# Which engine waits for the last stores: five semaphore waits moved from SP to TensorE at the end of an RMSNorm kernel

## Chip, cores and metric

One core of one Trainium2 chip. The metric is the device time of one execution in microseconds (us); lower is better. The groups of experiments ran on different chips, each together with the kernel before, so times are compared within a group; the short intervals that are read from traces are compared across groups as well.

Terms: the span is the time from the first to the last instruction of the program. A store has landed when the last of the 16 increments of its semaphore has come. In the lines of the profile, SPq, ACTq, DVEq and PEldq are the instruction queues of SP, ScalarE, VectorE and TensorE, and POOL is GpSimd.

## The reference

```python
def reference(x, gamma, eps):          # x: (16, 1024, 512) float32, gamma: ones(512), eps 1e-5
    rms = np.sqrt(np.mean(x ** 2, axis=-1, keepdims=True) + eps)
    x_norm = x / rms * gamma
    return np.maximum(x_norm, 0).astype(np.float32)
```

33.55 MB are read and 33.55 MB written, with little arithmetic on each element.

## The kernel before

Each of 128 partitions has 128 rows of 512 numbers. SP issues all 9 loads of x and all 7 stores, each with a semaphore of its own (`sems[m]`). GpSimd waits for the loads and passes the word on to ScalarE, which sums squares and takes the root; VectorE divides, scales and clips. TensorE computes nothing. Behind all work the semaphores that the program used are waited for and brought back to zero (a cut of the kernel; the comments are added here):

```python
    L, S = 0, 1
    room = nslots * K                                   # 6 * 16 = 96 rows of buffer
    order = [(L, 0, G), (L, G, G)] + [(L, i * K, K) for i in range(1, nslots)] + [
        (S, 0, K), (S, K, K), (L, room, K), (L, room + K, K),
        (S, 2 * K, 2 * K), (S, 4 * K, 2 * K), (S, room, K),
        (S, room + K, G), (S, room + K + G, G)]         # (kind, first row, rows); K = 16, G = 8
    # ... cut
    def take(engine, sem, n):
        engine.wait_ge(sem, n)
        engine.sem_inc(sem, -n)                         # built as one instruction: wait and subtract
    # ... cut: loads, stores, arithmetic
    take(nc.sync, done, ngroups)
    take(nc.sync, tick, ndyn)
    take(nc.sync, sq, ngroups - ndyn)
    take(nc.sync, sv, steps)
    take(nc.sync, sem_g, 16)
    for m, (kind, a, r) in enumerate(order):
        if kind == S and a + room >= rows:              # rows = 128: stores from row 32 on
            take(nc.sync, sems[m], 16)
```

The condition holds for five of the seven stores. The two earlier ones are waited for by SP before it reuses their buffers.

## Time and profile before

| kernel before | |
|---|---|
| time, median of 3 | 159.94 us (159.9 to 160.0) |
| span, first to last instruction | 158.6 us |
| time less span, profiled run | 1.32 us |
| DMA queue of SP | 98.6% of 16 engines' span, 67.11 MB |
| VectorE / ScalarE busy | 85% / 54% |
| last store: landing, SP's wait starts, ends | 158.563, 158.579, 158.596 us |

Transfers fill the span, so the span is set by them. The 1.32 us behind the span is the other part of the time, and the part that this change is about. The page doesn't show it, as no instruction of the program runs there. The trace's semaphore updates do. In what follows, "the walk" is a chain of nine steps of one semaphore that the trace lists (in the kernel before from 2.595 to 158.897 us): five up, read as the engines' reports, one after another, that they are through, and four back, read as the engines being let go in the reverse order. The trace doesn't name the engine of a step; what the reading rests on stands behind the prediction. There are two walks behind the kernel (the second from 159.682 to 160.039). "Resets" is the name for what lies between them: one more update each of over 200 semaphores, from 158.854 to 159.458 us; what these updates write is not recorded.

### The profile page before, as it was taken

What the parts mean: (1) busy time and instruction counts of PE and PEld (TensorE: products, weight loads), DVE (VectorE), ACT (ScalarE), POOL (GpSimd) and SP (SyncE); (2) the same over time, 40 slices, a digit from 0 to 9 for tenths busy, and PEclk for the clock granted to TensorE, in tenths of its full rate; (3) what the DMA queues carried; (4) which work ended last, traced back from release to release, by engine and by line L of the source; (5) the groups of instructions that cost most, each with busy time, mean ns of one, the idle gap of its engine ahead of it and who ended that gap; (6) DMA issues with size and microseconds to landing.
All of it is one profiled execution on the core that took longest, in us unless ns stands there. A gap on an engine that the chain in (4) does not pass through costs nothing.

```text
span 158.6 us, 770 instructions
## 1 busy us (share of the span) xinstructions
DVE 135.2 (85%) x76; ACT 86.3 (54%) x273; POOL 0.8 (0%) x6
## 2 busy tenths in 40 slices
DVE  0014999999999999999979999999999999999910
ACT  0388929889889989988920098898600000000000
POOL 1000000000000000000000000000000000000000
DMA  6999999999999999999999999997969969999997
GB/s 190 411 450 422 512 397 397 463 463 397 405 504 413 397 413 504 405 397 463 463 397 397 446 479 397 529 463 331 529 298 496 529 264 529 397 397 397 455 405 331
DMA packets 2312, 67.12 MB, mean 423 GB/s; under 512 B 260, under 2 KB 260, under 8 KB 264
## 3 DMA queue, kind: packets, MB, share of 16 engines
q1 hardware_dynamic: 2304, 67.11, 98.6%
q10 hardware_dynamic: 8, 0.01, 0.0%
HBM read 33.56 MB, written 33.55 MB: 423 GB/s over the span
## 4 chain that ended last, share of the span: by engine, by line
DVE 44%; ACT 27%; issue 6%; ACTq 4%; DVEq 0%; POOLq 0%
ACT junk L131 26%; DVE slots L185 22%; DVE slots L168 22%; ACTq L131 3%; ACTq L126 1%; DVE rstd L168 0%; ACT rms L136 0%; ACTq L136 0%; ACTq L139 0%; DVEq L181 0%; POOLq L118 0%
## 5 line engine op out<-in xcount | busy, mean ns | idle before, releaser
L131 ACT ACTIVATE junk<-slots 128x512 f32 x128 | 74.4, 581 | 21.7 <-POOLq L118 17.2
L185 DVE CUSTOM_DVE_ANT_1 slots<-slots,gamma_sb 128x8192 f32<-128x8192 f32 (+1 forms) x6 | 43.5, 7269 | 0.6
L168 DVE TENSOR_TENSOR slots<-slots,rstd 128x8192 f32<-128x8192 f32 x5 | 43.4, 8689 | 0.1
L154 DVE SCALAR_TENSOR_TENSOR slots<-slots,rstd,gamma_sb 128x512 f32 x48 | 32.3, 747 | 0.9 <-DVE rstd L149 0.9
L131 ACT ACTIVATION_READ_ACCUMULATOR junk<-slots x128 | 23.9, 187 | 0.0
L161 DVE TENSOR_SCALAR slots<-slots x6 | 13.8, 2294 | 0.2
L142 DVE LOAD_MASK_SELECT gamma_sb<-gseed x1 | 0.0, 14 | 8.2 <-DMA gseed<-in_gamma_dram 8.2
L136 ACT ACTIVATE rms<-ss,eps_sb x16 | 4.8, 301 | 1.8
L149 DVE RECIPROCAL rstd<-rms x6 | 1.2, 196 | 5.1 <-ACT rms L136 5.1
L124 ACT ACT_TABLE_LOAD x1 | 1.3, 1283 | 4.0 <-issue 4.0
L168 DVE RECIPROCAL rstd<-rms 128x32 f32<-128x32 f32 (+1 forms) x3 | 0.9, 315 | 0.9 <-ACT rms L136 0.9
L142 DVE STREAM_SHUFFLE gamma_sb<-gseed 128x512 f32<-128x512 f32 x1 | 0.7, 721 | 0.0
L113 POOL MEMSET gseed<- 128x512 f32 x1 | 0.5, 524 | 1.9 <-POOLq L98 1.9
L214 POOL MEMSET const-uint8-127<- 128x1 uint8 x1 | 0.1, 102 | 0.0
L214 POOL MEMSET const-bfloat16-1.0<- 128x1 bf16 x1 | 0.1, 101 | 0.0
L214 POOL MEMSET const-float32-0.0<- 128x1 f32 x1 | 0.1, 98 | 0.2 <-issue 0.2
L114 POOL MEMSET eps_sb<- 128x1 f32 x1 | 0.1, 99 | 0.0
L214 POOL MEMSET const-float32-1.0<- 128x1 f32 x1 | 0.1, 98 | 0.0
## 6 DMA issues: line engine op xcount, KB each, us to landing
slots<-in_x_dram SPq DMA_DIRECT2D x7, 4096.0 KB, 29.6
out_dram<-slots SPq DMA_DIRECT2D x3, 4096.0 KB, 15.0
slots<-in_x_dram SPq DMA_DIRECT2D x2, 2048.0 KB, 9.5
out_dram<-slots SPq DMA_DIRECT2D x2, 2048.0 KB, 7.1
out_dram<-slots SPq DMA_DIRECT2D x2, 22.2
gseed<-in_gamma_dram ACTq DMA_DIRECT2D x1, 8.0 KB
```

The costliest lines, as they stand in the source:

```text
L113: nc.gpsimd.memset(gseed, 0.0).then_inc(sem_z, 1)
L124: nc.scalar.preload_act_table(ACTF.Sqrt)
L126: with nc.scalar.Fori(0, ngroups) as gi:
L131: a = nc.scalar.activation(out=junk[:, j, :], in_=slots[:, bass.ds(base + j * d, d)], func=ACTF.Square, accum_out=ss[:, bass.ds(col + j, 1)])
L136: nc.scalar.activation(out=rms[:, bass.ds(col, G)], in_=ss[:, bass.ds(col, G)], func=ACTF.Sqrt, bias=eps_sb, scale=inv_d).then_inc(sq, 1)
L142: nc.vector.stream_shuffle(gamma_sb, gseed, [0] * 32)
L149: nc.vector.reciprocal(out=rstd[:, bass.ds(col, G)], in_=rms[:, bass.ds(col, G)]).then_inc(sv, 1)
L154: r = nc.vector.scalar_tensor_tensor(out=row, in0=row, scalar=rstd[:, bass.ds(col + j, 1)], in1=gamma_sb, op0=ALU.mult, op1=ALU.mult)
L161: nc.vector.tensor_scalar_max(out=blk, in0=blk, scalar1=0.0).then_inc(done, 1)
L168: emit(**kw).then_inc(sv, 1)
L185: nc.vector._custom_dve(dve_ops.TENSOR_MUL_SAT, out=blk, in0=blk, in1=gamma_sb[:, None, :].to_broadcast([P, r, d]), s0=float("inf"), s1=0. ...
L214: nc = _bacc.Bacc("TRN2", target_bir_lowering=False, num_devices=1)
```

## The change

Its intent: SP, which issues the transfers, is rid of the last waits, and TensorE, which has nothing to do, takes them. (The words that came with it speak of two stores; five waits move.)

```diff
     take(nc.sync, sem_g, 16)
     for m, (kind, a, r) in enumerate(order):
         if kind == S and a + room >= rows:
-            take(nc.sync, sems[m], 16)
+            take(nc.tensor, sems[m], 16)
```

## The prediction

> **What bounds the kernel now.** I read three things in order: the page, to see which engine or queue is full; the groups of instructions by line, to see what the moved waits are and how long each takes; and the trace's list of semaphore updates, to see what still runs after the last instruction of the program. The time before is 159.94 us (median of 3, 159.9 to 160.0), the profiled run took 159.92 us, and its span from first to last instruction is 158.6 us.
>
> The page, first the slices and the queues, then the issues:
>
> ```profile
> span 158.6 us, 770 instructions
> DVE 135.2 (85%) x76; ACT 86.3 (54%) x273; POOL 0.8 (0%) x6
> ...
> DVE  0014999999999999999979999999999999999910
> ...
> DMA  6999999999999999999999999997969969999997
> ...
> q1 hardware_dynamic: 2304, 67.11, 98.6%
> ...
> out_dram<-slots SPq DMA_DIRECT2D x2, 2048.0 KB, 7.1
> ```
>
> The DMA row is full nearly from end to end, and the queue that SP issues on is busy for 98.6% of the span over 16 engines: 67.11 MB at 423 GB/s is 158.6 us. VectorE, the next busiest, has 85% and does nothing in the last slice. TensorE has no row at all: it does no work. So the transfers set the time, and at the very end it is one transfer, the last 2 MB store. The stretches of the end show it:
>
> ```profile
> core 0: us, DVE busy (x) ACT busy (x) POOL busy (x), PEclk, DMA share, GB/s
> ...
> 142.50:151.20 8.70, 8.65 (x2) 0.00 (x0) 0.00 (x0) 1.00 0.96 414
> 151.20:158.60 7.40, 0.00 (x0) 0.00 (x0) 0.00 (x0) 1.00 0.85 363
> ```
>
> From 151.2 us on nothing computes; only bytes move, for 7.4 us. What waits for them is SP, in the line that the helper for "wait and subtract" has. The waits of SP's queue in the last 9 us, then the durations of that line, and of the barrier line at the start, the only place where TensorE runs an instruction of the same kind:
>
> ```profile
> SPq L87 <- SPq L87: 6.5, 2, 4.9
> ...
> L87 SPq EVENT_SEMAPHORE  x12: 17/17/17, 71.2 to 158.6; - x12
> ...
> L98 SPq EVENT_SEMAPHORE  x2: 17/17/17, 2.0 to 2.3; - x2
> ...
> L98 PEldq EVENT_SEMAPHORE  x2: 51/51/51, 2.0 to 2.3; - x2
> ```
>
> In the first line SP waits for 6.5 us in two pieces, the longest 4.9 us: these are the two last stores. (The view names SP's own line as the releaser since SP issued those stores.) The other lines give the price of one wait-and-subtract: 17 ns on SP, 51 ns on TensorE.
>
> **After the last instruction.** The time is 1.32 us longer than the span (159.92 less 158.6). The trace's semaphore updates go on there, and I read them one by one. The last increments of the last store's semaphore come at 158.563; SP's wait starts at 158.579 and ends at 158.596. Then a semaphore that the program does not use is stepped: at 2.595, 113.911, 113.949, 151.299, 158.733, and at once back at 158.776, 158.814, 158.849, 158.897. Nine steps are five engines going up and four coming back. The first five match the times at which the engines run out of instructions: TensorE ends at 2.360, ScalarE at 113.763, GpSimd long before ScalarE, VectorE at 151.148, SP at 158.596. So the order is TensorE, ScalarE, GpSimd, VectorE, SP, and back; each must wait for the one ahead of it, and TensorE is let go last. After it come the resets of about 50 semaphores an engine (158.854 to 159.458; the last block, starting at 159.11, is the slow one, TensorE's), and a second walk of nine steps, from 159.682 to 160.039.
>
> [...]
>
> **The change part by part.** The words speak of two stores, but the condition (a + 96 at least 128) holds for five: the stores from rows 32, 64, 96, 112 and 120. So five waits leave SP and five appear on TensorE. No engine's transfers, arithmetic, or order of issue change, and no byte moves earlier or later.
>
> 1. Removed on SP: five instructions of 17 ns, about 67 ns apart. Four of them were past by 153.745, waiting for data, and only the last lies on the end: 16 ns from landing to start, and 17 ns of execution.
> 2. Added on TensorE: it is through with the opening barrier at 2.36 us and then parks on the first of the five semaphores. Those fill at about 119.8, 139.1, 148.8, 153.7 and 158.56 us, so again only the last is on the end. It starts at about 158.59: in the opening barrier TensorE woke 11 ns later than SP (0.661 against 0.650), so I add 11 to SP's 158.579. It ends 51 ns later, 158.64. The span should thus read 158.64, 0.045 more.
> 3. From the last instruction to the engine's step in the walk: SP needed 0.137 (158.596 to 158.733), TensorE 0.235 (2.360 to 2.595). TensorE steps at about 158.876.
> 4. The walk. Before, the late engine was the last of the chain: the way up was done and only the way back was left, 0.164 us (158.733 to 158.897). Now the late engine is the first: all of the way up is still to do, then the way back. The whole walk is seen twice in this trace with nobody late: the second one behind the kernel, 159.682 to 160.039, is 0.357 us, and the last one before it, from -0.371 to 0, is 0.371. I take 0.364. The walk ends at 159.240 in place of 158.897.
> 5. What follows (resets, second walk) is the same and starts 0.343 later.
>
> Sum: (0.011 + 0.034) for the instruction, (0.235 - 0.137) = 0.098 for the way to the step, and (0.364 - 0.164) = 0.200 for the walk; together 0.343 us. 159.94 + 0.34 = 160.28 us, 0.2% slower.
>
> **Rivals.** (a) The walk is not in what is timed, or is not ordered as I read it: then only the slower instruction remains, +0.05 us, 159.99. For it: the page shows nothing of the walk. Against it: the time exceeds the span by 1.32 us, about what the walks and resets take. (b) SP, freed of its waits, is done at 151.9 and something starts earlier: a gain. Against it: SP has no store left to issue after 151.5, and the transfers end when the bytes have moved, so 159.94 or less by nothing. [...] (c) TensorE wakes slowly out of a wait of over 100 us, or the five waits delay each other. For it: it is the slowest sequencer here, 51 ns against 17. Against it: the last two stores land 4.8 us apart and the five cost well under 1 us if all were taken in a row; a slow wake of 0.5 us would make 160.8. (d) A last wait of another engine takes over. None can: the other engines end by 151.9.
>
> **Range and chances.** My point is 160.28. The low end, 160.0, takes in rival (a) with the scatter of 0.1 that the three runs show; the high end, 160.5, takes in 0.2 for a slower way from TensorE's last wait to the barrier[...]. Two per cent is 3.2 us, ten times the sum, and no part of the change reaches the transfers, so within 2% has 0.985, slower 0.01, faster 0.005.
>
> **What would show it.** Right: TensorE's sequencer has five more entries on the helper's line, 51 ns each, the last at about 158.59; SP's last entry is near 151.86; the span is 0.03 to 0.1 longer while the time grows by about 0.34, so that time less span goes from 1.3 to about 1.6; the step semaphore has its nine steps close together within 0.4 us after 158.8, rather than strung out from 2.6; the DMA rows and the busy times of VectorE and ScalarE stay within 0.3 us. Wrong: the first step still comes early (then TensorE is not the first of the walk), the time grows by no more than the span does (rival a), or TensorE's last wait starts over 0.1 us after the landing (rival c). If the stores themselves landed at another time, the change would act through the transfers, which nothing here foresees.

A paragraph and two single passages with statements that no trace of this case shows are cut out of the prediction. No term of its sum goes with them: 0.045 for the instruction, 0.098 for the way to the step and 0.200 for the walk are 0.343 us, and 159.94 + 0.34 is 160.28.

What its reading of the walk and the resets rests on, from the traces of before and of the changed kernel:

- The five steps up are put to the engines by the ends of their instructions, as the prediction says. That each waits for the one ahead shows in GpSimd, whose last instruction ends at 100.443 and whose step comes at 113.949, 0.038 us behind ScalarE's.
- The four steps back are put to VectorE, GpSimd, ScalarE and TensorE by the time from the step ahead: 0.043, 0.038 and 0.035 us for the first three, as those engines have on the way up in the second walk (0.044, 0.038 and 0.034).
- In the kernel before, the steps of the two walks that follow on at once are 23 to 48 ns apart, but for the turn behind SP's step in the second walk, 99 ns. In the changed kernel's first walk, where VectorE had made its own step only 24 ns ahead of SP's, the turn takes 97 ns; in the first walk of before, where VectorE's step was at 151.299, 43 ns.
- The resets come in five runs of consecutive semaphores, 42 to 49 of each recorded in the kernel before and 47 to 51 in the changed one. They begin 0.121, 0.151, 0.140, 0.116 and 0.213 us behind the fifth to ninth step of the first walk; in the changed kernel, where these steps lie otherwise, 0.117, 0.149, 0.141, 0.115 and 0.215. So each run of resets is put to the engine of its step. TensorE's takes 0.348 us, SP's 0.087.
- SP's last wait lasted 4.9 us and is recorded with 17 ns.
- From the last landing (158.563) to the time of the profiled run (159.92) are 1.36 us: 0.33 to the end of the first walk, 0.56 to the end of the resets, the rest most of the second walk.

## The result

| | before | changed |
|---|---|---|
| median, us | 159.97 (159.9 to 160.29, 6 runs) | 160.38 (160.26 to 160.62, 6 runs) |
| ratio | | 1.0025 (95%: 1.0012 to 1.0038) |
| span, profiled run | 158.6 | 158.8 |

Ratios here are the mean time of one kernel's fast runs over that of the other's of the same rounds, so not quite the ratio of the medians. The change is 0.4 us slower, a quarter of a per cent, and within the 2% that count as the same.

The page of the changed kernel, in the lines that answer to those shown of before:

```profile
span 158.8 us, 770 instructions
...
DVE 135.2 (85%) x76; ACT 86.3 (54%) x273; POOL 0.8 (0%) x6
...
DVE  0013999999999999999979999999999999999910
...
DMA  5999999999999999999999999997979969999997
...
q1 hardware_dynamic: 2304, 67.11, 98.5%
...
out_dram<-slots SPq DMA_DIRECT2D x2, 2048.0 KB, 7.1
```

Nothing that works has changed: the same 770 instructions, the same busy times, the same queue, and the same 7.1 us from issue to landing of a 2 MB store. The stretches of the changed kernel's end, set at its own times (VectorE ends at 151.33, the span at 158.8):

```profile
core 0: us, DVE busy (x) ACT busy (x) POOL busy (x), PEclk, DMA share, GB/s
142.70:151.35 8.65, 8.63 (x2) 0.00 (x0) 0.00 (x0) 1.00 0.97 417
151.35:158.80 7.45, 0.00 (x0) 0.00 (x0) 0.00 (x0) 1.00 0.85 361
```

The last store again moves alone, at the same pace (361 GB/s, before 363). What has moved is on line 87, in the helper `take`, where every wait that is built with it shows (columns: engine, operation, how many; shortest, median and longest ns; first and last start in us):

```profile
L87 SPq EVENT_SEMAPHORE  x7: 17/17/17, 71.3 to 152.0; - x7
L87 PEldq EVENT_SEMAPHORE  x5: 51/51/51, 119.9 to 158.7; - x5
```

SP has 7 in place of 12 and is through at 152.0; TensorE's queue has 5, of 51 ns each. The longest waits of SP's queue show the same: "SPq L87 <- SPq L87" is now 21.6 us in two waits, where it was 28.2 us in four.

```profile
SPq L87 <- SPq L87: 21.6, 2, 12.0
```

And the semaphore updates behind the end, in us from the span's start, the first walk of both kernels (not a view of the profile, but the trace's own list):

```
          up: TensorE  ScalarE  GpSimd   VectorE  SP       back: VectorE  GpSimd   ScalarE  TensorE
before          2.595  113.911  113.949  151.299  158.733        158.776  158.814  158.849  158.897
changed       158.994  159.028  159.066  159.110  159.134        159.231  159.271  159.305  159.352
```

Before, four engines had already reported when the last store landed, and only SP's step and the way back were left. In the changed kernel TensorE, the first in the chain, is the late one, and all nine steps lie behind the landing. From the end of the first walk to the end of the second the two kernels take the same: 1.142 and 1.144 us.

From landing to the end of the first walk is 0.334 us before and 0.673 changed. The difference, 0.339, is the effect of the change. The six runs agree: their time less span averages 1.62 us, where the kernel before has 1.34 to 1.35 in all groups of runs below, 0.27 to 0.28 more; the rest, 0.047, lies inside the span, since the last wait starts 13 ns later after the landing and lasts 34 ns longer. The remaining 0.12 between the two profiled runs (159.92 and 160.38) lies ahead of it: the last store landed at 158.563 in the one and at 158.679 in the other. The loads differ already near the start (the first one landed at 8.05 and at 8.21), where the two kernels are alike.

### The profile page after: what moved, and what is told of

The parts are those of the page before. It is cut to its first block, busy times and chain, and to the rows that moved or that the text cites. A ratio compares the mean times of both kernels' runs of the same rounds, so it can differ in the third digit from the quotient of the medians.

```text
span 158.8 us, 770 instructions
## 1 busy us (share of the span) xinstructions
DVE 135.2 (85%) x76; ACT 86.3 (54%) x273; POOL 0.8 (0%) x6
## 4 chain that ended last, share of the span: by engine, by line
DVE 44%; ACT 26%; issue 6%; ACTq 4%; DVEq 0%; POOLq 0%
ACT junk L131 26%; DVE slots L185 22%; DVE slots L168 22%; ACTq L131 3%; ACTq L126 1%; DVE rstd L168 0%; ACT rms L136 0%; ACTq L136 0%; ACTq L139 0%; DVEq L181 0%; POOLq L118 0%
```

## The experiments

Theory A: the cost is the late engine's place in the walk, plus its own pace from landing to its step. Theory B: only TensorE's slow handling of the wait (51 ns against 17) costs anything, and the place doesn't matter. Besides, the surplus of the medians (0.41 against a sum of 0.34) had to be put down to scatter or to the transfers.

Since landings scatter by some tenths between runs (the spans of the kernel before go from 158.6 to 159.1 us), each kernel is read in two ways: from its trace, landing of the last store to end of the first walk; and over all its runs, the mean of time less span. Spans are listed to 0.1 us, so a mean over 5 to 11 runs is good to a few hundredths. Kernel before, in the three groups of runs: time less span 1.35, 1.34 and 1.34; its mean times 160.15, 160.21 and 160.16.

**All five waits on ScalarE.**

```diff
-            take(nc.sync, sems[m], 16)
+            take(nc.scalar, sems[m], 16)
```

> All five last waits on ScalarE, the second engine of the walk. Theory A (place in the walk): from the landing of the last store to the end of the first walk 0.016 + 0.017 + 0.148 (ScalarE's last instruction to its step, as in the kernel before) + 0.323 (0.357 of a whole walk less the 0.034 step from TensorE) = 0.504 us, against 0.334 with SP: time +0.17 us. Theory B (only TensorE's slow sequencer costs): same as before, within 0.03.

Measured: ratio 1.0015 (1.0001 to 1.0028), mean 160.34; landing to end of walk 0.507; time less span 1.52, 0.17 more than before. The helper's lines:

```profile
L87 SPq EVENT_SEMAPHORE  x7: 17/17/17, 71.2 to 151.8; - x7
L87 ACTq EVENT_SEMAPHORE  x6: 17/17/17, 4.1 to 158.7; - x6
```

ScalarE executes the wait in 17 ns like SP, and it still costs 0.17 us. TensorE's step is at 2.596, ScalarE's at 158.838, then the others follow in 0.324. Theory B falls, theory A has its number to 3 ns.

**All five on GpSimd.** The same edit with `nc.gpsimd`.

> All five last waits on GpSimd, the third engine. Theory A: 0.016 + 0.017 + about 0.14 + 0.285 (0.357 less 0.034 and 0.038) = 0.458 us from landing to the end of the walk: time +0.12 us. Theory B: same as before, within 0.03.

Measured: ratio 1.0041 (1.0027 to 1.0054); landing to end of walk 0.889 where 0.458 was expected; time less span 1.87.

```profile
L87 POOLq EVENT_SEMAPHORE  x14: 17/17/17, 8.1 to 159.0; - x14
```

A miss. The walk from GpSimd's step on took 0.286, as expected (0.285); the surplus is in the term that had been borrowed from other engines: from the end of GpSimd's wait (159.031) to its step (159.593) are 0.562, not 0.14.

**All five on VectorE.** The same edit with `nc.vector`.

> All five last waits on VectorE, the fourth engine. Theory A: 0.016 + 0.021 + 0.151 + 0.241 (0.357 less 0.116) = 0.43 us from landing to the end of the walk: time +0.10 us. Theory B: same as before, within 0.03.

Measured: ratio 1.0043 (1.003 to 1.0057); landing to end of walk 0.473, near the 0.43 (the way to VectorE's step took 0.183 and not 0.151, the start 0.027 and not 0.016); but time less span 1.85.

```profile
L87 DVEq EVENT_SEMAPHORE  x5: 21/21/21, 142.4 to 159.2; - x5
```

A miss in the total. It lies in the second walk: VectorE's way back comes 0.499 after SP's step (160.537 to 161.036), where the kernel before has 0.099 and the changed one 0.099. All five runs have it: time less span 1.82 to 1.91. (Both these kernels' spans also average 0.14 and 0.22 above those of before in the same rounds, 158.94 and 159.02 against 158.80. Spans of one kernel vary by up to 0.7, and I leave that open.)

**Only the last store's wait on TensorE.**

```diff
-            take(nc.sync, sems[m], 16)
+            take(nc.tensor if m == len(order) - 1 else nc.sync, sems[m], 16)
```

> Only the last store's wait on TensorE, the four earlier ones back on SP. If just the last of the five lies on the end: the whole effect of the change, 0.67 us from landing to the end of the walk, time +0.34 us as in the changed kernel (ratio about 1.0021). Rival (the five waits on TensorE delay each other): visibly less than the changed kernel, by up to four times 0.15 us.

Measured: ratio 1.0027 (1.0013 to 1.0041), mean 160.53, 0.38 over before; landing to end of walk 0.712; time less span 1.67. The same view, the helper's line by engine:

```profile
L87 SPq EVENT_SEMAPHORE  x11: 17/17/17, 71.2 to 153.7; - x11
...
L87 PEldq EVENT_SEMAPHORE  x1: 51/51/51, 158.6 to 158.6; - x1
```

One wait brings the whole effect, and the rival that five delay each other falls. The 0.04 above the changed kernel is in one term: from the wait's end to TensorE's step are 0.275, against 0.235 in the kernel before, the changed one and its repetition. Why is open.

**Only the first four on TensorE.** The same line with the two engines exchanged.

> The four earlier stores' waits on TensorE, the last one back on SP. If just the last wait counts: same as before within 0.05 us, SP's landing to end of the walk 0.33 us, since TensorE is through at about 153.9. If five moved waits share the cost: four fifths of the change, +0.27 us.

Measured: ratio 1.0 (0.9987 to 1.0013); landing to end of walk 0.334; time less span 1.31. The helper's line in this kernel:

```profile
L87 SPq EVENT_SEMAPHORE  x8: 17/17/17, 71.2 to 158.7; - x8
L87 PEldq EVENT_SEMAPHORE  x4: 51/51/51, 119.9 to 153.9; - x4
```

Four of the five moved instructions cost nothing: TensorE's step is at 154.146, long before SP's at 158.864. Together with the last experiment this settles that the last wait alone counts.

**All five on TensorE, the last store's first.**

```diff
-    for m, (kind, a, r) in enumerate(order):
+    for m, (kind, a, r) in reversed(list(enumerate(order))):
         if kind == S and a + room >= rows:
-            take(nc.sync, sems[m], 16)
+            take(nc.tensor, sems[m], 16)
```

> All five on TensorE, the last store's taken first, so that the other four, long fulfilled, are executed behind the last landing. TensorE's spacing estimated from the opening barrier, 51 ns of execution and 100 ns to the next: four more cost 0.60 us on top of the change, time +0.94 us over before. If waits already fulfilled cost nothing: as the changed kernel, +0.34.

Measured: ratio 1.0059 (1.0046 to 1.0072), mean 161.19, 0.98 over before; landing to end of walk 1.320, 0.647 more than in the changed kernel. The view of the cores (span and granted clock), then TensorE's part of the helper's line:

```profile
core 0: 159.6 us, clock 1.000
```

```profile
L87 PEldq EVENT_SEMAPHORE  x5: 51/51/51, 158.9 to 159.6; - x5
```

Now all five lie behind the landing, from 158.95 to 159.65: 0.15 us from start to start on TensorE (one of the four distances was 0.195). A wait that is already fulfilled was not free here, at 0.15 us; the same four cost nothing (ratio 1.0) in the experiment before, where they were passed while the last store was awaited.

**The same reversal on SP.** Only the first changed line of the last diff.

> The same reversal on SP: four more instructions about 67 ns apart behind the last landing, +0.27 us over before. If fulfilled waits cost nothing: same as before within 0.03.

Measured: landing to end of walk 0.600, 0.266 more than before; ratio 1.0025 (1.0012 to 1.0038), mean 160.58, 0.37 over before where 0.27 was expected; one run with a span of 159.7 weighs in it, and without that run it is 0.28. SP's part of the helper's line:

```profile
L87 SPq EVENT_SEMAPHORE  x12: 17/17/17, 71.2 to 159.0; - x12
```

SP's five are 66 to 68 ns apart (158.763 to 159.030), less than half of TensorE's distance.

**The changed kernel once more.**

> The changed kernel again, for the 0.41 us between the medians against the 0.34 of the sum. If the surplus is scatter of when the stores land: the part from landing to the end of the walk is again 0.67 us, and the difference of the means lies near 0.34. If the change also delays the transfers: the last landing is again 0.1 us later than in the kernels with SP's wait, in every run.

Measured: ratio 1.0018 (1.0005 to 1.0031), mean 160.53 against 160.21, a difference of 0.32; landing to end of walk 0.670. Its spans average 158.90, those of before in the same rounds 158.87. Less the 0.047 by which TensorE's instruction starts and ends later, that is no delay of the transfers. The profiled run's own last landing, 158.906, was later still than in the first two (158.563 and 158.679), but the spans of the kernel before reach 159.1 in these rounds, so it says nothing of the change. That the surplus of the first result was scatter of the landings fits all this, though it isn't shown, as the spans of the first six runs of before weren't recorded. The effect is 0.34, and the two comparisons gave 0.40 and 0.32.

The two misses, GpSimd and VectorE, were looked into with the last four runs. Theory G: what was seen belongs to the engine. Theory F, a guess: it is one stop of about 0.4 us (0.42 and 0.40 over what was expected of the two) at a fixed count of instructions on that engine, which happened to fall there.

**Only the last store's wait on GpSimd.**

```diff
+            take(nc.gpsimd if m == len(order) - 1 else nc.sync, sems[m], 16)
```

> Only the last store's wait on GpSimd, four instructions fewer ahead of the barrier than with all five. With five, GpSimd needed 0.562 us from its last wait to its step, about 0.42 more than ScalarE (0.145) did. Theory G (GpSimd is always that slow to reach the walk): again about 0.56 us, time less span about 1.87. Theory F (a single stop of about 0.4 us at a fixed count of instructions, which happened to fall there): the step comes after about 0.14 us; the stop may show up at a later step of GpSimd's or nowhere on the end, time less span then 1.45 (or 1.87 if it falls in the walks).

Measured: 0.562 again (158.700 to 159.262), landing to end of walk 0.887, time less span 1.89, ratio 1.0033 (1.0019 to 1.0048).

**All five on GpSimd, eight spare increments at its start.**

```diff
+    pad = nc.alloc_semaphore("pad")
+    for step in (1, -1):
+        for _ in range(4):
+            nc.gpsimd.sem_inc(pad, step)
```

> All five waits on GpSimd, and eight increments of a spare semaphore (sum zero) at its start, where it waits anyway. Theory G: 0.56 us from the last wait to the step as without them, time less span 1.87. Theory F: the stop falls eight instructions earlier, into the time in which GpSimd is parked on stores; the step comes after 0.14 us, landing to end of the first walk 0.46, time less span 1.45, as theory A said of this engine at first.

Measured: 0.561 (159.128 to 159.689), landing to end of walk 0.889, time less span 1.88, ratio 1.0032 (1.0019 to 1.0045). With one, five, and thirteen added instructions GpSimd needs the same 0.56 us. Theory G holds for GpSimd, and F falls. Why GpSimd is that slow isn't shown.

**Only the last store's wait on VectorE.** As above, with `nc.vector`.

> Only the last store's wait on VectorE. With five, the way back from SP in the second walk took 0.499 us in place of 0.099. Theory G (an effect of VectorE having waited last): again about 0.5 there, time less span about 1.85. Theory F (a stop at a fixed count of instructions): that step is back at 0.1, the sum from landing to the end of the first walk stays near 0.47, time less span near 1.45, unless the stop falls on another step of the walks.

Measured: the way back in the second walk 0.098, landing to end of the first walk 0.478, time less span 1.45, ratio 1.0007 (0.9994 to 1.002). VectorE's part of the helper's line:

```profile
L87 DVEq EVENT_SEMAPHORE  x1: 21/21/21, 158.7 to 158.7; - x1
```

**All five on VectorE, eight spare increments at its start.**

> All five waits on VectorE, and eight such increments at its start, where it waits for gamma anyway. Theory G: 0.5 us again for the way back from SP in the second walk, time less span 1.85. Theory F: the stop falls eight instructions earlier, ahead of the second walk, where VectorE has slack while TensorE's resets run; the way back is 0.1, time less span near 1.45.

Measured: 0.099, 0.479, time less span 1.44, ratio 1.0011 (0.9997 to 1.0024). For VectorE theory G falls: of the three counts tried, the stop came with five added instructions, and neither with one nor with thirteen, while the late engine was the same. That fits F, a stop that depends on how many instructions stand ahead. What stops there isn't shown. From the span's start on, the transfer lists of the three kernels with waits on VectorE show one packet of the instruction queue, in the padded kernel alone, of 8192 bytes, from 158.065 to 158.374 us, while VectorE was parked on the last store's wait:

```profile
q14 instruction: 1, 0.01, 0.0%
```

But the list doesn't say which engine the packet was for, and in no kernel was any transfer recorded behind the last store, where the stop lies. So no run here ties the packet to the stop, and the cause stays open. (The slack of VectorE that the expectation speaks of: in the changed kernel the resets put to it end at 159.691 us, those put to TensorE at 159.914.)

No kernel beat the one before; of the engines tried, SP is the cheapest to be late (by the traces and by time less span; for VectorE with the last wait alone, the ratio of the times can't tell it from SP).

## Why the prediction was right

The time on record was 160.28 with a range of 160.0 to 160.5; the first six runs had a median of 160.38, the repetition one of 160.56 beside a kernel before that was then at 160.18. It was right on the size of the change, by these steps:

1. *Only the last of five waits lies on the end.* Shown: alone on TensorE it brought 0.38 us, the other four alone a ratio of 1.0.
2. *The instruction, 0.011 and 0.034.* TensorE started 29 ns after the landing, SP 16 ns: 13 in place of 11. Its 51 ns against 17 are exact.
3. *The way to the step, 0.098.* 158.759 to 158.994 are 0.235 against SP's 0.137: exact, read off the opening of the trace of before. TensorE is the first in the chain and waits for nobody there, so that its 0.235 stood bare in that trace. (The prediction calls the lines of L98 the only place where TensorE runs such an instruction; line 214 has one more, also of 51 ns, and the prediction itself uses its start, 0.661.)
4. *The walk, 0.200.* Whole walk 0.358 against 0.364 taken: 0.194.
5. *What follows is the same.* 1.142 and 1.144 us.

The sum is 0.339 in place of 0.343. Rival (a), that the walks aren't timed, falls: in the profiled runs of both kernels and all twelve experiments the last step of the second walk, counted from the span's start, stands 0.115 to 0.123 us above the reported time, while it moved from 160.039 to 161.389. Rival (b), a gain by freeing SP, falls with the first four waits moved at no gain. Rival (c), a slow wake or mutual delay, falls with the 29 ns and the fourth experiment; the five waits in a row, there an estimate, took 0.70 us in the reversed kernel. Rival (d) needed another engine later than 158 us, and none was.

Of its signs, one holds in part: the span was to be 0.03 to 0.1 longer. In the same rounds it is 0.03 longer (158.90 against 158.87); between the two profiled runs it is 0.16, of which 0.116 is the later landing.

What the prediction did not size well is the noise. It took the scatter for 0.1 us from three runs of before; later runs of the same kernel went from 159.92 to 160.45, so the range left little room: the repetition's median lies above it, though its difference to the kernel before, 0.32, is near the one foreseen. That the first median lies within the range is thus in part luck; that the difference was met is not.

The terms, in one table: from landing to the end of the first walk with one engine late, in us, each from one profiled run.

| late engine | landing to start | execution | end to its step | rest of the walk | sum | less SP |
|---|---|---|---|---|---|---|
| SP (before) | 0.016 | 0.017 | 0.137 | 0.164 | 0.334 | |
| VectorE (last wait only) | 0.028 | 0.021 | 0.188 | 0.241 | 0.478 | 0.144 |
| ScalarE (all five) | 0.021 | 0.017 | 0.145 | 0.324 | 0.507 | 0.173 |
| TensorE (changed) | 0.029 | 0.051 | 0.235 | 0.358 | 0.673 | 0.339 |
| GpSimd (last wait only) | 0.024 | 0.017 | 0.562 | 0.284 | 0.887 | 0.553 |

The column of the walk follows the place in the chain, and gives TensorE more than half of its 0.339 (0.194). The column of the step is a matter of the engine, and there GpSimd is the odd one. Over all profiled runs the end to the step took 0.136 to 0.137 us on SP, 0.145 to 0.148 on ScalarE, 0.151 to 0.188 on VectorE, 0.235 to 0.275 on TensorE and 0.56 on GpSimd in three kernels; the walk from the late engine's step on took 0.284 to 0.286 for GpSimd and 0.241 to 0.242 for VectorE.

The step that failed in the experiments' expectations was the same for two engines: the time from an engine's last instruction to its step was assumed for GpSimd (0.14, measured 0.56), since in the trace of before GpSimd's step waits for ScalarE's and hides it.

## What to carry to other kernels

An idle engine was not a free engine here: whoever was last to finish decided how much of the closing chain was still ahead (0.164 us behind SP, 0.358 behind TensorE), so leave the wait for the last transfer to the engine that stands last in it, and let it be that engine's last instruction. On a kernel of 160 us this is worth a fifth of a per cent; of a shorter kernel the same 0.34 us would be a larger share, but none was run here. And look behind the span for what a change at the very end does: the time less the span was steadier than the time itself (of the kernel before 1.34 to 1.35 in three groups of runs, with mean times of 160.15 to 160.21), and showed here in five runs what the times alone blurred.
